# A second chunk of gate and up by seven block products, at 1.25 half-steps a turn, in a four-layer trunk on one core

## The chip, the core and the metric

The program runs on one core of a Trainium2 chip. The metric is the device time of one execution in microseconds. Engines: PE (TensorE, matmuls) with PEld (its weight loads), DVE (VectorE), ACT (ScalarE), POOL (GpSimd) and SP (SyncE, which issues most DMAs). Each engine works through its own instructions in program order and waits on semaphores for the others.

## The reference

A trunk of 4 layers on x of shape (1, 256, 1024) in float32. Each layer is a feed-forward block, a mixer, and a second feed-forward block:

```python
x = x + 0.5 * swiglu(rms_norm(x, g0), w_gate, w_up, w_down)   # 1024 -> 2816 -> 1024
x = x + mixer(rms_norm(x, g1))        # conv, attention (MLA), spatial gating, conv
x = x + 0.5 * swiglu(rms_norm(x, g2), w_gate, w_up, w_down)
# swiglu(x) = (silu(x @ w_gate) * (x @ w_up)) @ w_down
```

The attention mixer is causal softmax attention with 16 heads over low-rank queries and keys (w_uq, w_ukv) and an output matrix w_o. All weights are float32 and every matrix is read once.

## The kernel before, in words

**Precision.** Every float32 product is made of three matmuls. A weight tile is split into a high part (`whi`, a copy on ScalarE, L112) and a low part (`wlo`, a subtraction on VectorE, L123); activations likewise (L291, L292). `products` (L333, L334, L336) then adds high x high, high x low and low x high in PSUM.

**Rows and streams.** The 256 rows are two tiles t = 0 and t = 1 of 128 rows. `stream(t)` is a Python generator that goes through all twelve blocks. `advance(t)` takes one step of it; here one such call is named a turn. The loop at the end (L1281 to L1288) lets t = 0 go `LAG` = 4 turns ahead and then takes t = 1 and t = 0 alternately. The order of instructions on every engine is the order of these calls; nothing is reordered later. `later(n, f)` runs f after n more turns.

**Weight units.** `unit` asks `Weights.get` for a piece of 1024 columns in all (two rows of tiles by 512 columns). Both tiles use one unit; it is made when t = 0 asks for the unit `AHEAD` = 4 places before it (3 while activations are on their way, `CHAIN_AHEAD`). `make` issues the copy on ScalarE in that turn, `complete` the subtraction on VectorE at the start of the next turn, and then SP may load a further raw tile (`N_RAW` = 6 buffers). A plain turn of the feed-forward block is one unit: six matmuls of 512 columns.

**Feed-forward block** (`ffn`, L503). Columns of gate and up come in chunks 0 to 4 of 512 and chunk 5 of 256. For a plain chunk, each tile takes 4 turns of gate and 4 of up (chunk 0 and the gate of chunk 1 go together, in 12 turns: first half of the contraction, then the second). When up is done, `up_done` (L525) multiplies (L532), transposes 32 by 32 (L534) on VectorE, and after every second chunk sends the result through DRAM (`Turned`), from where `read` (H_READ = 7 turns before its use) and `take` (H_TAKE = 2 turns before) bring it back as the left operand of down. The products with down follow in `rows_into_x`; the chunk done by seven products comes last there.

**Seven products.** Except in the very first block, chunk 4 of both tiles is computed as a 2 x 2 block product (rows: the two tiles; contraction: two halves of 512; columns: two halves of 256) with seven block products in place of eight. This is the generator `sevens` (L606), called a lane. It needs sums of activation blocks (`form`, L621), sums of weight blocks (`sum_of`, L650), high and low parts of them (`high` L626, `low` L631), and 12 matmuls of 256 columns per product (L764). One matrix (gate or up) of a chunk is called a unit of the lane here and has steps q = 0 to 6. A product takes two half-steps. The first (up to the `yield` at L752) issues for VectorE the subtraction for the next product, the sum for the one after it, and small additions (L686) that join results; the second issues the 12 matmuls and ScalarE's copy for the product after the next. Five half-steps stand ahead of the first product. Banks y, z, x of PSUM are reused: at q = 6 VectorE reads z (L751, through L686) before the seventh product adds to it.

**Pace of the lane.** The lane is opened when t = 1 enters the block, and starts once all activations are taken. In each turn `beside` (L1271) adds `RATE` = 0.6 to a credit and takes one half-step if the credit has reached 1. `follow` (L580) brings t = 1 up to one turn behind t = 0 at turn 10 of t = 0 (t = 0 stands still for three rounds), and back to four when the lane ends. `load_first` loads the first four weight blocks during the mixer or the block before; further blocks are loaded at q = 4 and q = 5 of the unit before into a pool of four buffers.

**Activations between blocks.** `prepare_x` (L432) sends half of x through DRAM (write, four reads) and takes it `X_TAKE` = 12 turns later on ScalarE (L443, L291) and VectorE (L292).

**Attention.** `mla` (L1051): `keys`, then four `queries`, each with a unit of w_uq (asking four ahead, so units of w_o are made there too), then scores with Exp (L1187), values and the output product.

**Start.** `start` issues 4 warm-up matmuls and, three turns later, `WARM[1]` = 6 more.

## Time and profile before

| | us |
|---|---|
| three runs, median (lowest to highest) | 1853.66 (1853.48 to 1860.08) |
| the profiled execution, its time | 1853.95 |
| its span, first to last instruction | 1852.2 |

The time of an execution is some 1.75 us over its span. In a row of a timeline the first number is the start in us from the span's start, the second the duration; then engine, line, operation, tile written and tiles read, and how many in a row (x4). What stands in brackets is the idle time of the engine just before, and what ended it. Matmuls are pipelined: the spacing of their starts tells their cost, not the duration shown.

### The profile page before, as it was taken

Reading aid. Unit: us, or ns where it says so; the run is one execution under the profiler, and the core shown is the slowest. Engines: PE = TensorE matmul, PEld = TensorE weight load, DVE = VectorE, ACT = ScalarE, POOL = GpSimd, SP = SyncE. Lnnn points to the kernel's source line nnn. Section 1 sums busy time; section 2 is a strip of 40 time slices with the busy share of each in tenths; the row PEclk is TensorE's granted clock in tenths of the full one; section 3 lists DMA queues with packets and bytes.
Section 4 is the critical chain, followed back from the end, with each engine's and each line's share of the span. In section 5 each row is a group of like instructions: output and inputs, shape, how many; then the busy total and the mean of one; then the engine's idle time right before and its main releaser. Section 6 shows DMA issues by size and latency. Waiting matters only on the chain.

```text
span 1852.2 us, 24827 instructions
## 1 busy us (share of the span) xinstructions
PE 1826.1 (99%) x9022; PEld 1521.3 (82%) x9022; DVE 1286.6 (69%) x1574; ACT 988.7 (53%) x1421; POOL 144.7 (8%) x279
## 2 busy tenths in 40 slices
PE   9999999999999989999999999999999999999999
PEld 7888887888888868888878888888888888878887
DVE  5555677776687666686668665778667775777773
ACT  5344545554655486554565456565456554546452
POOL 2000101000530151100010001100000000000000
PEclk9999999999999998999999999999999999999999
DMA  7678666669766841676976786656786777766674
GB/s 265 218 237 238 215 222 199 215 190 293 230 208 204 250 151 58 195 226 192 272 237 220 216 261 204 225 177 225 236 265 202 227 233 230 236 205 188 218 232 132
DMA packets 251612, 400.36 MB, mean 216 GB/s; under 512 B 25415, under 2 KB 116449, under 8 KB 251489
## 3 DMA queue, kind: packets, MB, share of 16 engines
q1 hardware_dynamic: 250480, 397.09, 68.0%
q8 instruction: 70, 1.15, 0.3%
q0 software_dynamic: 608, 1.11, 0.2%
q10 hardware_dynamic: 400, 0.57, 0.1%
q14 instruction: 54, 0.43, 0.1%
HBM read 365.67 MB, written 33.03 MB: 215 GB/s over the span
## 4 chain that ended last, share of the span: by engine, by line
PE 90%; DVE 3%; ACT 2%; DMA 2%; issue 2%; SPq 0%; ACTq 0%; DVEq 0%
PE acc L334 27%; PE acc L336 27%; PE acc L333 27%; PE acc L764 7%; PE tr L299 1%; DMA xturn<-s 1%; DVE wlo L123 1%; ACT whi L112 1%; PE acc L1206 1%; PE acc L1179 1%; DMA raw<-in_ffn_gate_dram 1%; DVE wlo L631 0%; ACT whi L626 0%; DVE s L803 0%; SPq L468 0%
## 5 line engine op out<-in xcount | busy, mean ns | idle before, releaser
L333 PE MATMUL acc<-whi,s 128*128 128x512 f32 (+2 forms) x2440 | 937.8, 384 | 2.4 <-ACT s L291 1.7
L334 PE MATMUL acc<-wlo,s 128*128 128x512 f32 (+2 forms) x2440 | 932.8, 382 | 2.7 <-DVE wlo L123 2.7
L336 PE MATMUL acc<-whi,s 128*128 128x512 f32 (+2 forms) x2440 | 896.5, 382 | 0.0
L123 DVE TENSOR_TENSOR wlo<-raw,whi 128x1024 fp32r<-128x1024 f32 (+1 forms) x580 | 685.7, 1208 | 100.9 <-ACT whi L112 98.4
L112 ACT ACTIVATE whi<-raw 128x1024 fp32r<-128x1024 f32 (+1 forms) x580 | 588.1, 1044 | 87.3 <-DMA raw<-in_ffn_down_dram 43.7
L336 PEld LDWEIGHTS acc<-whi,s 128*128 128x128 f32 x2440 | 459.1, 188 | 96.8 <-DVE s L292 1.0
L334 PEld LDWEIGHTS acc<-wlo,s 128*128 128x128 f32 x2440 | 459.4, 188 | 95.7 <-DVE wlo L123 6.9
L333 PEld LDWEIGHTS acc<-whi,s 128*128 128x128 f32 x2440 | 459.2, 188 | 92.8 <-ACT s L291 2.8
L626 ACT ACTIVATE whi<-block 128x1024 fp32r<-128x1024 f32 x98 | 103.4, 1055 | 130.6 <-DVE block L650 130.6
L764 PE MATMUL acc<-whi,s 128*128 128x256 f32 x784 | 155.4, 281 | 7.5 <-DVE s L686 7.5
L764 PEld LDWEIGHTS acc<-whi,s 128*128 128x128 f32 x784 | 127.0, 188 | 14.2 <-DVE s L686 10.5
L631 DVE TENSOR_TENSOR wlo<-block,whi 128x1024 fp32r<-128x1024 f32 x98 | 118.7, 1212 | 1.2 <-ACT whi L626 0.3
L292 DVE TENSOR_TENSOR s<-s,s 128x512 fp32r<-128x512 f32 (+1 forms) x58 | 39.9, 688 | 113.7 <-ACT s L291 112.3
L523 ACT ACTIVATE s<-acc,evened 128x512 f32<-128x512 f32 (+1 forms) x70 | 44.9, 641 | 128.0 <-PE acc L336 125.8
L411 POOL TENSOR_TENSOR total<-ss,ss 128x1 f32<-128x1 f32 x26 | 8.0, 306 | 1308.2 <-ACT s L402 1308.2
L764 PE MATMUL acc<-wlo,s 128*128 128x256 f32 x392 | 110.0, 281 | 0.0
L402 ACT ACTIVATE s<-x 128x512 bf16<-128x512 f32 x48 | 30.3, 630 | 133.3 <-DVE x L426 98.3
L325 DVE TENSOR_TENSOR s<-big,s 128x512 fp32r<-128x512 f32 x68 | 46.2, 680 | 77.6 <-ACT s L324 74.9
L532 DVE SCALAR_TENSOR_TENSOR s<-acc,evened,s 128x512 f32<-128x512 f32 (+1 forms) x70 | 48.5, 693 | 64.3 <-PE acc L336 64.3
L426 DVE SCALAR_TENSOR_TENSOR x<-acc,x 128x512 f32<-128x512 f32 x32 | 22.0, 689 | 79.8 <-PE acc L336 79.7
L764 PEld LDWEIGHTS acc<-wlo,s 128*128 128x128 f32 x392 | 73.7, 188 | 3.7
L650 DVE TENSOR_TENSOR block<-block,block 128x1024 f32<-128x1024 f32 x56 | 68.4, 1221 | 1.0
(151 smaller groups left out, 904.4 us busy)
## 6 DMA issues: line engine op xcount, KB each, us to landing
raw<-in_ffn_down_dram SPq DMA_DIRECT2D x176, 512.0 KB, 5.8
raw<-in_ffn_gate_dram SPq DMA_DIRECT2D x148, 512.0 KB, 4.5
raw<-in_ffn_up_dram SPq DMA_DIRECT2D x148, 512.0 KB, 4.6
raw<-in_conv_w_in_dram SPq DMA_DIRECT2D x48, 512.0 KB, 5.0
turn<-big SPq DMA_DIRECT2D x32, 512.0 KB, 3.1
big<-turn SPq DMA_DIRECT2D x128, 128.0 KB, 5.9
block<-in_ffn_gate_dram SPq DMA_DIRECT2D x28, 512.0 KB, 6.1
block<-in_ffn_up_dram SPq DMA_DIRECT2D x28, 512.0 KB, 6.7
```

Of the source, the lines that this page charges most:

```text
L112: self.nc.scalar.activation(hi[:, part], self.loaded[u][:, part], AF.Copy)
L123: self.nc.vector.tensor_tensor(out=lo[:, part], in0=src[:, part], in1=hi[:, part].bitcast(F32), op=ALU.subtract)
L325: nc.vector.tensor_tensor(out=lo.rearrange("p k (i b) -> p k i b", b=32), in0=src, in1=hi.bitcast(F32).rearrange("p k (i b) -> p k i b", b ...
L333: nc.tensor.matmul(ps, lhsT=ah[:, k, :], rhs=wh[:, wk, c], start=first, stop=False)
L334: nc.tensor.matmul(ps, lhsT=ah[:, k, :], rhs=wl[:, wk, c], start=False, stop=False)
L336: nc.tensor.matmul(ps, lhsT=al[:, k, :], rhs=wh[:, wk, c], start=False, stop=last)
L523: nc.scalar.activation(sg[n], ps[:, :w], AF.Silu, scale=r)
L532: nc.vector.scalar_tensor_tensor(out=h, in0=ps[:, :w], scalar=r, in1=sg[n], op0=ALU.mult, op1=ALU.mult)
L626: nc.scalar.activation(hi, src, AF.Copy)
L631: nc.vector.tensor_tensor(out=lo, in0=src, in1=hi.bitcast(F32), op=ALU.subtract)
L650: nc.vector.tensor_tensor(out=to, in0=to, in1=raws[u][added[q]], op=ALU.add)
L764: nc.tensor.matmul(ps[:, :256], lhsT=f[:, k, :], rhs=w[:, k, :], start=q in (0, 1, 3) and k + n == 0, stop=k == 3 and n == 2, skip_group_c ...
```

## The change

Chunk 3 joins chunk 4 in the lane (four units in place of two), and the lane takes 1.25 half-steps a turn, so in every fourth turn two. The four raw blocks get a buffer each, by a table that turns with every unit, so that each block of the next unit goes into the buffer that is freed first: block 11 is loaded at q = 3, 12 and 22 at q = 4, 21 at q = 5. Chunks of the lane are read 4 turns before use. Plain chunk 2 is now paired with chunk 5 on its way through DRAM, where one buffer is added. In attention, t = 0 calls Exp once on a scrap element after its normalization; the queries ask for fewer units ahead (4, 3, 2, 1), and units of w_o are made between the scores of t = 0. The second warm-up has 3 matmuls in place of 6.

```diff
-N_SEVENS_RAW = 4
-N_DRAM = 4
+N_DRAM = 5
-H_READ, H_TAKE = 7, 2
-SEVENS, RATE = (4,), 0.6
+H_READ, H_TAKE, SEVENS_READ = 7, 2, 4
+SEVENS, RATE = (3, 4), 1.25
-WARM = (4, 6)
+WARM = (4, 3)
-    sevens_pool = ctx.enter_context(tc.tile_pool(name="sevens", bufs=N_SEVENS_RAW))
+    sevens_pool = ctx.enter_context(tc.tile_pool(name="sevens", bufs=1))
-    def unit(t, m, k, n, c0, width):
+    def unit(t, m, k, n, c0, width, ahead=AHEAD):
...
-        return W.get((m, k, n, c0, width, copy), AHEAD if not any(in_chain) else CHAIN_AHEAD)
+        return W.get((m, k, n, c0, width, copy), min(ahead, AHEAD if not any(in_chain) else CHAIN_AHEAD))
...
-            events.setdefault(at - H_READ, []).append(lambda n=n: read(n))
+            events.setdefault(at - (SEVENS_READ if n in seven else H_READ), []).append(lambda n=n: read(n))
...
+    buffers = {"21": 0, "11": 1, "12": 2, "22": 3}
+    def next_buffers():
+        buffers.update({"11": buffers["21"], "12": buffers["11"], "22": buffers["12"], "21": buffers["22"]})
...
-        raw = sevens_pool.tile([P, 4, 256], F32, tag="block", name=name("block"))
+        raw = sevens_pool.tile([P, 4, 256], F32, tag=f"block{buffers[name_]}", name=name("block"))
...
-        for n, block in enumerate(("11", "12", "22", "21")):
+        for n, block in enumerate(("21", "11", "12", "22")):
...
+            if q == 3:
+                next_buffers()
+                load(u + 1, "11")
             if q == 4:
-                load(u + 1, "11", "12")
+                load(u + 1, "12", "22")
             if q == 5:
-                load(u + 1, "22", "21")
+                load(u + 1, "21")
...
     def mla(t, i, ib, shared, then):
         a, r = yield from normed(t, IDLE_MLA)
+        if t == 0:
+            nc.scalar.activation(tiny(1, "scrap", 1), half, AF.Exp)
...
-            queries(b, unit(t, ("w_uq", ib), 0, 2, 384 * b, 384))
+            queries(b, unit(t, ("w_uq", ib), 0, 2, 384 * b, 384, 4 - b))
...
             later(S_TURN[t], lambda h0=h0, p=p: values(h0, p))
+            if t == 0 and h0 >= 4:
+                W.make()
...
         credit[0] += RATE
-        if credit[0] >= 1:
+        while lanes and credit[0] >= 1:
             credit[0] -= 1
```

## Rows read from the trace of the kernel before

**Rows 1.** The page, part 1: busy time of each engine.

```profile
PE 1826.1 (99%) x9022; PEld 1521.3 (82%) x9022; DVE 1286.6 (69%) x1574; ACT 988.7 (53%) x1421; POOL 144.7 (8%) x279
```

**Rows 2.** The page, part 4: the chain that ended last, by engine.

```profile
PE 90%; DVE 3%; ACT 2%; DMA 2%; issue 2%; SPq 0%; ACTq 0%; DVEq 0%
```

**Rows 3.** Busy time by stretch; columns: us, PE, PEld, DVE, ACT, POOL, PEclk, DMA share, GB/s.

```profile
1410.00:1445.00 35.00, 35.00 (x177) 29.51 (x176) 34.44 (x39) 20.96 (x27) 0.00 (x0) 1.00 0.64 201
```

**Rows 4.** Timeline of TensorE: a product's first matmul, then plain ones.

```profile
1419.63 0.28 PE L764 MATMUL acc<-whi,s 128*128 128x256 f32 x1
...
1421.06 0.39 PE L333 MATMUL acc<-whi,s 128*128 128x512 f32 x1
...
1423.84 0.39 PE L333 MATMUL acc<-whi,s 128*128 128x512 f32 x1
```

**Rows 5.** Timeline of VectorE in the same lane.

```profile
1416.62 0.69 DVE L621 TENSOR_TENSOR s<-s,s 128x512 f32<-128x512 f32 x1
1417.22 1.22 DVE L631 TENSOR_TENSOR wlo<-block,whi 128x1024 fp32r<-128x1024 f32 x1
...
1434.14 1.22 DVE L123 TENSOR_TENSOR wlo<-raw,whi 128x1024 fp32r<-128x1024 f32 x1
1435.28 0.74 DVE L532 SCALAR_TENSOR_TENSOR s<-acc,evened,s 128x512 f32<-128x512 f32 x1
1436.05 0.71 DVE L534 STREAM_TRANSPOSE big<-s 128x512 f32<-128x512 f32 x1
1436.69 1.18 DVE L123 TENSOR_TENSOR wlo<-raw,whi 128x1024 fp32r<-128x1024 f32 x1
```

**Rows 6.** Turn 0 in timelines and chain: sixth lane; then the first lane.

```profile
1404.70 0.69 ACT L523 ACTIVATE s<-acc,evened 128x512 f32<-128x512 f32 x1 [1.83 <-PE acc L336]
1409.42 0.69 DVE L292 TENSOR_TENSOR s<-s,s 128x512 fp32r<-128x512 f32 x1 [5.67 <-ACT s L291]
1419.80 1.42 PE acc L764 x12
...
311.43 0.69 DVE L292 TENSOR_TENSOR s<-s,s 128x512 fp32r<-128x512 f32 x1 [6.65 <-ACT s L291]
324.11 1.42 PE acc L764 x12
```

**Rows 7.** Waits of TensorE (total us, times, longest), then timelines at a seventh product.

```profile
PE acc L764 <- DVE s L686: 7.5, 7, 1.1
...
1456.74 0.41 DVE L686 TENSOR_TENSOR s<-acc,s 128x256 f32<-128x256 f32 x1
1457.21 0.38 PE L764 MATMUL acc<-whi,s 128*128 128x256 f32 x1 [1.04 <-DVE s L686]
```

**Rows 8.** Loads of the lane's weight blocks, 512 KB each.

```profile
DMA to landing us min/median/max: 4.8/6.5/9.0
```

**Rows 9.** Attention: timelines of ScalarE and TensorE, then stretches as in rows 3.

```profile
683.19 1.04 ACT L112 ACTIVATE whi<-raw 128x1024 fp32r<-128x1024 f32 x1
704.18 1.28 ACT L1187 ACT_TABLE_LOAD   x1 [0.76 <-DVE nb L1184]
694.38 1.06 PE L299 MATMUL tr<-ident,s 128*96 128x128 f32 x4 [2.19 <-DVE s L1049]
694.00:696.00 2.00, 1.62 (x7) 1.60 (x8) 1.97 (x5) 1.97 (x5) 1.11 (x2) 0.61 0.03 10
696.00:698.00 2.00, 2.00 (x10) 1.81 (x9) 1.90 (x8) 1.12 (x2) 0.50 (x2) 0.54 0.60 134
```

**Rows 10.** Timeline of the start: second warm-up, then a weight's low part.

```profile
6.09 2.67 PE L266 MATMUL acc<-ident_r 128*128 128x512 f32 x6
7.62 1.28 DVE L123 TENSOR_TENSOR wlo<-raw,whi 128x512 fp32r<-128x512 f32 x2
```

**Rows 11.** DMA issues: kind, count, size each, median us from issue to landing.

```profile
turn<-big SPq DMA_DIRECT2D x32, 512.0 KB, 3.1
...
s<-turn SPq DMA_DIRECT2D x56, 64.0 KB, 4.4
```

## The prediction

> **What bounds the kernel now.** I read the engines' busy time first: TensorE is busy 99% of the span, VectorE 69%, ScalarE 53% [rows 1]. The chain of waits agrees: nine tenths of it is TensorE [rows 2]. So the kernel is a queue of matmuls, and leaving matmuls out is worth their spacing, as long as nothing else ends last. Whether that holds must be read from the stage in which the change puts work, the first part of a feed-forward block, where one chunk runs by seven products beside the plain chunks. There, over 35 us in a row, VectorE is busy 34.4 us [rows 3]. The average of 69% hides a stage in which VectorE is full and TensorE is kept fed only because every product is asked for late.
>
> A turn is one call of `advance`; I number turns from turn 0, in which the last half of the activations is taken and the generator `sevens` (the lane) may begin.
>
> **Matmuls: less.** Twelve plain matmuls of 512 columns start over 2.78 us, 0.232 us each; the twelve of a product, 256 columns, take 1.43 us to the next start [rows 4]. A chunk of gate and up costs 96 x 0.232 = 22.2 us plain and 14 x 1.43 = 20.0 us by products. It saves 2.2 us in each of the seven blocks that have a lane: **15.5 us**. The Trainium skill (TensorE: Matmul & The Clock Gate, "Back-to-back issue gap") speaks against this: sustained streams are given as 131 ns at 512 columns and 81 ns at 128; an estimate on the line between, 98 ns at 256, makes it 14 x 12 x 98 ns = 16.5 us against 12.6 us, a loss of 27 us over seven blocks. The trace shows both shapes, and in it the small one takes half the time of the large one; the measurement decides, and I give that case no chance.
>
> **VectorE: more, and sooner.** From start to start, a subtraction or sum of 1024 elements takes 1.14 us, one of 512 elements 0.60 us, an up chunk's product and transpose 0.77 + 0.64 us [rows 5]. A chunk by products needs 14 subtractions and 8 sums of 1024 where a plain one needs 8 subtractions: 14 x 1.14 = 16 us more per block. Spread evenly it fits. At 1.25 half-steps a turn, a turn holds 1.39 + 0.625 x 1.43 = 2.28 us of TensorE; VectorE has half a weight unit's subtraction (0.57), an up chunk's share (0.18) and 0.625 of a product's share (1.14 + 4/7 x 1.14 + about 0.35 for the operations of 256 elements, taken at half the price of 512; 2.14 in all), so 2.09 us, 92%. What decides is the beginning, where it isn't spread evenly.
>
> Start of the lane. TensorE ended turn 0 when ScalarE's wait in the 1404.70 row ended, while VectorE, held in order behind the activations' trip through DRAM, reached turn 0's subtraction at 1409.42 [rows 6]. The first product is the lane's seventh half-step. At 0.6 it falls in turn 11, at 1.25 in turn 5: six turns or 6 x 1.39 = 8.3 us earlier. Over the seven blocks that subtraction starts 10.4 (the worst) to 12.7 us ahead of the first product, 11.9 in the mean (both ends: [rows 6]), so the new first product is asked for about 3.5 us after it. By then VectorE must have done that subtraction, five operations of 512, two weight units' subtractions and the first block's, 0.6 x 5 to 6 + 3 x 1.14 = 6.5 us: a wait of 3.0 us in the mean, 2.3 to 4.6.
>
> It doesn't end there. The seventh product writes a bank that VectorE reads in the half-step before it (L751), and in VectorE's order that read stands behind the next unit's first subtraction and sum. Even now TensorE waits for it once per block, 7 times 1.1 us at most [rows 7]. At the new rate it is asked for at turn 15: 3.5 + 10 x 1.39 + 6 x 1.43 = 26.0 us after the subtraction of turn 0. Up to and with that read VectorE has: 0.61, eight operations on activations (4.9), eight blocks' subtractions (9.1), six sums (6.8), six weight units (6.8: t = 0 stands still three rounds), two up chunks (2.8), two of 256 elements (0.7) = 31.8 us, and one gap of 1.2 us where a sum must pass ScalarE before its subtraction. 33.0 - 26.0 = 7.0 us, in which the 3.0 are contained; 1.0 of it is paid today. So 6.0 us more per block, **+42 us**; without the gap 4.8 (34 us), with a late block load 6.5 (46 us).
>
> Later units. There are three such unit ends per block in place of one. At the second, count from the end of turn 19, the last matmul of t = 0's second up chunk: VectorE has two up chunks, three blocks, two sums and two weight units, 2 x 1.41 + 7 x 1.14 = 10.8 us; then the freed buffer is loaded, 6.5 us [rows 8]; then sum and read, 1.5 us: 18.8. TensorE has seven turns and four products, 15.5. The bounds are 0 (VectorE comes early, having caught up at the wait before) and 3.3 us; I take 2.0, since the wait before lets it catch up in part: **+14 us** over seven blocks. At the third no up chunk stands in that stretch, and I take 0, with up to 1.5 us for the bound.
>
> **The other edits.** In the attention block ScalarE's chain ends last. Three copies of output weights of 1.04 us leave it, and the table load before the first Exp, 1.28 us, goes to an earlier turn where ScalarE idles; but one of TensorE's waits there, 2.19 us, is for VectorE [rows 9]. Bounds: 0 and 3.1 + 1.3 + 1.3 us (a slow stretch of the clock less). I take the load and half of the copies: **-2.9 us**. The copies land among the scores, where ScalarE waits for VectorE anyway. The Trainium skill (ScalarE: Activation LUTs, "What ACT_TABLE_LOAD costs") counts 2.66 us for a switch, with the drain; this trace shows only the load's row, and by the page the sum would be 1.4 us lower. The three warm-up matmuls less save nothing: the first real ones wait for the low part of their weights, ready after 8.2 us [rows 10]. The later reads of turned chunks (4 turns before use, 2 before the take, at 1.39 us and two streams 5.6 us) give a little less than four issues and 4.4 us to landing take [rows 11], so ScalarE may wait half a microsecond; four weight units made ahead cover it. The read that now follows its write by one turn holds SP's queue for about 3.1 us [rows 11]; six raw buffers cover that; without them it costs 3.1 us per tile. The new block order and the fifth DRAM buffer cost nothing by themselves.
>
> **Sum**, against the profiled execution's 1853.95 us, 0.3 above the median: 1853.95 - 15.5 - 2.9 + 42 + 14 = 1891.5 us, so about **1891 us**.
>
> **Rivals.**
> 1. Faster: VectorE's lead holds. Then 1853.95 - 15.5 - 2.9 = 1835.5 us, 1826 to 1844 with the bounds. For it: in the stage now TensorE loses hardly anything though VectorE is full [rows 3], and on average 92% fits. Against: the order count above. It decides if the subtraction of turn 0 starts some 7 us sooner against TensorE, for example because the activations come back from DRAM earlier. Chance 0.22.
> 2. No change: only the first product waits (7 x 3.0 = 21 us), and VectorE catches up before the seventh: 1853.95 - 18.4 + 21 = 1856.5 us. It needs 4 us of slack in VectorE's order that I don't find. Chance 0.10.
> 3. Slower still, by the clock: after a wait of 2.19 us the granted clock fell to 0.61 and 0.54 in the next 2 us stretches, near the lower of its levels, 1.2 GHz [rows 9]. By those two rows a wait of that length costs 2 x 0.39 + 2 x 0.46 = 1.7 us more. Inside the first unit that is hidden, since VectorE ends last there; behind two unit ends per block it isn't: 1891 + 14 x 1.7 = 1915 us. Chance 0.08.
> 4. The lane does not run at that rate, or the second chunk stays plain: impossible to tell from times alone, but the counts would show it. Chance under 0.01.
>
> **Numbers.** The forecast has 0.60, its own range 1866 (42 -> 34, 14 -> 0) to 1912 (42 -> 46, 14 -> 23, and some 8 at the third unit's end). About 0.5%, 9 us, is what a measurement can tell from no change. Faster 0.22, same 0.10, slower 0.68 (cases 3 and forecast). The range 1836 to 1915 takes in half of case 1 and leaves out its lower half and a little above.
>
> **What would show it.** Plain matmuls of 512 columns fall by 224 on each of L333, L334, L336, and the products' matmuls go from 1176 to 2352. TensorE should wait at the first product of every lane 2 to 5 us for VectorE's subtraction (L631), and some 3 us at the seventh for L686; VectorE should be full for some 60 us from each lane's start. In the attention block the table load should stand before the scores. If TensorE's waits on L764 come to less than 15 us in all, my count of VectorE's order is wrong, and the time is near 1836.

## The result, and the profile after

The changed kernel takes 1943.3 us (median of 4 runs, 1939.4 to 1954.1) where the kernel before took 1855.1 us beside it: a ratio of 1.048, with 1.046 to 1.050 as its 95% interval. That is 88 us slower. The forecast was slower by 37 us; the sign was right and the size was not, and the time lies outside the range. The profiled execution has a span of 1942.7 us, 90.5 us more than before. All line numbers below are those of the kernel after unless said otherwise: the products' matmuls are L772 (before L764), the plain ones L332, L333 and L335, VectorE's low form of a weight block L636, its sum L655, its read of a product's bank L691, ScalarE's snapshot of a bank L687, an up chunk's product and transpose L531 and L533.

The page of the kernel after, busy time and chain of waits by engine, against [rows 1] and [rows 2]:

```profile
PE 1845.5 (95%) x9523; PEld 1552.5 (80%) x9523; DVE 1415.5 (73%) x1721; ACT 1040.9 (54%) x1513; POOL 146.4 (8%) x279
...
PE 39%; DVE 11%; DMA 5%; ACT 4%; issue 3%; SPq 1%; POOL 0%; ACTq 0%; DVEq 0%
```

The shares of the kernel after add up to only 63% of the span, where those before add up to all of it: this chain was not followed back to the start. Of the part that was followed, TensorE has about six tenths (39 of 63) where it had nine, and VectorE 17% (11 of 63) where it had 3%. TensorE no longer ends everything. The groups of the page show that the change did what it says (count behind the x, then busy time and mean ns, then idle time before):

```profile
L332 PE MATMUL acc<-whi,s 128*128 128x512 f32 (+3 forms) x2216 | 854.5, 386 | 4.5 <-ACT whi L111 2.7
L772 PE MATMUL acc<-whi,s 128*128 128x256 f32 x1568 | 324.3, 289 | 54.4 <-DVE s L691 41.1
L772 PE MATMUL acc<-wlo,s 128*128 128x256 f32 x784 | 226.0, 288 | 19.1 <-DVE wlo L636 19.1
```

The plain matmuls went from 2440 to 2216 on each line and the products' to 1568 + 784 = 2352, both as forecast. The idle time is at the products. TensorE's waits (total us, times, longest), where before there was the one line of [rows 7]:

```profile
PE acc L772 <- DVE s L691: 41.1, 21, 3.7
PE acc L772 <- DVE wlo L636: 19.1, 9, 3.2
PE acc L772 <- ACT s L687: 13.3, 19, 1.2
```

These three are 73.5 us, against 7.5 us before. Where in a lane they stand is read from the timeline of TensorE, here the first of the seven lanes: first product (two rows), then the seventh, the fourteenth and the twenty-first, each the last of a unit of seven.

```profile
316.56 0.28 PE L772 MATMUL acc<-whi,s 128*128 128x256 f32 x1
318.94 0.39 PE L772 MATMUL acc<-wlo,s 128*128 128x256 f32 x1 [2.10 <-DVE wlo L636]
...
345.06 0.39 PE L772 MATMUL acc<-whi,s 128*128 128x256 f32 x1 [0.46 <-DVE s L691]
...
373.70 0.38 PE L772 MATMUL acc<-whi,s 128*128 128x256 f32 x1 [2.13 <-DVE s L691]
...
402.95 0.39 PE L772 MATMUL acc<-whi,s 128*128 128x256 f32 x1 [3.73 <-DVE s L691]
```

Over the seven lanes the first product waits 2.08 to 3.21 us, the seventh 0.43 to 0.48, the fourteenth 0.93 to 2.21 and the twenty-first 3.68 to 3.73; the twenty-eighth, which ends the lane, doesn't wait. A wait of the trace is a little less than what is lost: in the first two rows the starts are 2.38 us apart where 0.12 us is usual, so 2.26 us are lost for 2.10 shown, 0.16 us more at every wait.

The longest wait takes the clock with it. Two stretches of the kernel after, around the twenty-first product (columns as in [rows 3]; PEclk is the third from the right):

```profile
400.00:405.00 5.00, 2.05 (x13) 2.05 (x14) 4.96 (x6) 2.34 (x3) 0.00 (x0) 0.90 0.82 297
405.00:410.00 5.00, 5.00 (x35) 5.00 (x34) 1.39 (x2) 0.99 (x3) 0.00 (x0) 0.76 0.34 108
```

TensorE stood idle for 3.73 us, VectorE was full, and then the granted clock fell to its lower level: 0.10 x 5 + 0.24 x 5 = 1.7 us of TensorE's time are lost. I call 1 less the granted clock, summed over stretches of 1 us, the lost clock. Within the span it is 32.4 us in the kernel after (mean clock 0.983) and 7.2 us before (0.996); an expectation below counts 18.0 us for a run that has 17.1, because it goes past the last instruction. Of the 32.4, 23.9 lie in the lanes, 14 falls of 1.7 us: 7 behind the twenty-first product, one in every lane; 6 behind the first product, in five lanes; 1 behind a fourteenth. The other 8.5 lie in the attention part.

### The profile page after: what moved, and what is told of

It is laid out like the page before. It is cut to its first block, busy times and chain, and to the rows that moved or that the text cites. A ratio compares the mean times of both kernels' runs of the same rounds, so it can differ in the third digit from the quotient of the medians.

```text
span 1942.7 us, 26046 instructions
## 1 busy us (share of the span) xinstructions
PE 1845.5 (95%) x9523; PEld 1552.5 (80%) x9523; DVE 1415.5 (73%) x1721; ACT 1040.9 (54%) x1513; POOL 146.4 (8%) x279
## 3 DMA queue, kind: packets, MB, share of 16 engines
q8 instruction: 74, 1.21, 0.3%
## 4 chain that ended last, share of the span: by engine, by line
PE 39%; DVE 11%; DMA 5%; ACT 4%; issue 3%; SPq 1%; POOL 0%; ACTq 0%; DVEq 0%
PE acc L335 10%; PE acc L332 10%; PE acc L333 10%; PE acc L772 6%; DVE wlo L636 3%; DVE block L655 2%; DVE wlo L122 2%; DMA block<-in_ffn_gate_dram 1%; DMA block<-in_ffn_up_dram 1%; ACT whi L111 1%; DMA xturn<-s 1%; PE tr L298 1%; DMA raw<-in_ffn_down_dram 1%; DVE s L531 1%; ACT whi L631 1%
## 5 line engine op out<-in xcount | busy, mean ns | idle before, releaser
L332 PE MATMUL acc<-whi,s 128*128 128x512 f32 (+3 forms) x2216 | 854.5, 386 | 4.5 <-ACT whi L111 2.7
L333 PE MATMUL acc<-wlo,s 128*128 128x512 f32 (+3 forms) x2216 | 847.9, 383 | 2.7 <-DVE wlo L122 2.7
L335 PE MATMUL acc<-whi,s 128*128 128x512 f32 (+3 forms) x2216 | 811.8, 382 | 0.0
L122 DVE TENSOR_TENSOR wlo<-raw,whi 128x1024 fp32r<-128x1024 f32 (+2 forms) x524 | 620.7, 1208 | 63.5 <-ACT whi L111 63.4
L111 ACT ACTIVATE whi<-raw 128x1024 fp32r<-128x1024 f32 (+2 forms) x524 | 530.6, 1042 | 76.7 <-DMA raw<-in_ffn_down_dram 49.2
L335 PEld LDWEIGHTS acc<-whi,s 128*128 128x128 f32 x2216 | 420.4, 190 | 89.2 <-DVE s L324 2.3
L332 PEld LDWEIGHTS acc<-whi,s 128*128 128x128 f32 x2216 | 422.0, 190 | 84.6 <-ACT whi L111 4.5
L333 PEld LDWEIGHTS acc<-wlo,s 128*128 128x128 f32 x2216 | 421.3, 190 | 81.5 <-DVE wlo L122 5.5
L772 PE MATMUL acc<-whi,s 128*128 128x256 f32 x1568 | 324.3, 289 | 54.4 <-DVE s L691 41.1
L631 ACT ACTIVATE whi<-block 128x1024 fp32r<-128x1024 f32 x196 | 207.0, 1056 | 286.1 <-DVE block L655 279.7
L772 PEld LDWEIGHTS acc<-whi,s 128*128 128x128 f32 x1568 | 261.6, 194 | 76.8 <-DVE s L691 48.6
L636 DVE TENSOR_TENSOR wlo<-block,whi 128x1024 fp32r<-128x1024 f32 x196 | 237.2, 1210 | 46.9 <-ACT whi L631 46.2
L772 PE MATMUL acc<-wlo,s 128*128 128x256 f32 x784 | 226.0, 288 | 19.1 <-DVE wlo L636 19.1
L772 PEld LDWEIGHTS acc<-wlo,s 128*128 128x128 f32 x784 | 152.1, 194 | 26.9 <-DVE wlo L636 21.8
L655 DVE TENSOR_TENSOR block<-block,block 128x1024 f32<-128x1024 f32 x112 | 136.7, 1221 | 10.4 <-DMA block<-in_ffn_gate_dram 8.7
L323 ACT ACTIVATE s<-s 128x512 fp32r<-128x512 f32 x28 | 17.6, 630 | 86.0 <-DMA s<-turn 86.0
```

What stands on the lines that cost most here:

```text
L111: self.nc.scalar.activation(hi[:, part], self.loaded[u][:, part], AF.Copy)
L122: self.nc.vector.tensor_tensor(out=lo[:, part], in0=src[:, part], in1=hi[:, part].bitcast(F32), op=ALU.subtract)
L332: nc.tensor.matmul(ps, lhsT=ah[:, k, :], rhs=wh[:, wk, c], start=first, stop=False)
L333: nc.tensor.matmul(ps, lhsT=ah[:, k, :], rhs=wl[:, wk, c], start=False, stop=False)
L335: nc.tensor.matmul(ps, lhsT=al[:, k, :], rhs=wh[:, wk, c], start=False, stop=last)
L631: nc.scalar.activation(hi, src, AF.Copy)
```

## The experiments

Three theories stood at the start. **Order**: the loss is a read that frees a bank, standing behind other work in VectorE's order. **Total**: VectorE simply has too much to do in the lane, in whatever order. **Other edits**: part of the loss has nothing to do with the second chunk.

### The other edits alone

```
-SEVENS, RATE = (3, 4), 1.25
+SEVENS, RATE = (4,), 0.6
```

> The changed kernel with one chunk in the lane at 0.6 half-steps a turn again; block order, early Exp, output units, warm-up and DRAM buffer stay changed. Theory (the other edits are worth only the attention block's 2.8 us): 1851 us, within 4. Rival (one of them, such as the block loads or the later output units, carries part of the loss): 1862 or more.

Measured: 1870.5 us, ratio 1.009 (1.006 to 1.012). The rival was right: about 15 us come from the other edits. The lanes are as before, one wait of 1.06 us each. What is new are waits of plain matmuls, in TensorE's view of waits:

```profile
PE acc L332 <- ACT s L323: 6.8, 4, 3.8
```

and behind them, in ScalarE's view of the same run, a wait for a DMA (before, its waits for that read came to 15.4 us in 10):

```profile
ACT s L323 <- DMA s<-turn: 60.6, 14, 8.6
```

This is the turned chunk being read 4 turns ahead of its use in place of 7. Undoing that edit on top of the first run:

```
-H_READ, H_TAKE, SEVENS_READ = 7, 2, 4
+H_READ, H_TAKE, SEVENS_READ = 7, 2, 7
```

> One chunk by seven products at 0.6 half-steps a turn with all other edits, as in the run of the other edits alone (1870.5 us), but the turned tiles of the product chunk are read again 7 turns ahead of their use, as before the change, in place of 4. Theory: the 15 us that the other edits cost are mostly this read: ScalarE waits for its DMA (60.6 us in 14 waits there, longest 8.6), the split that a plain matmul needs comes late (6.8 us in 4 waits of the matmuls at L332), and the granted clock falls after the longest of them (3.4 us lost at 454 to 462). With 7 turns the four waits go and that fall with them: 1860 us (1857 to 1864). Rival: the order of the weight units in the attention layer and the order of the block loads carry the loss, and the read is hidden: 1868 to 1872, with the waits at L332 below 3 us all the same.

Measured: 1857.6 us (10 runs), ratio 1.001 (1.000 to 1.002). As the theory said: the waits for L323 are gone from TensorE's list, ScalarE's waits for the read are 14.9 us, and the time is that of the kernel before. This run still has the edits of the attention part, so with one chunk all edits but the later read come to between 0 and 4.5 us together; what each gives or costs is not told apart. By the two medians the later read costs 13 us with one chunk; the four times of the first run spread over 12 us (1867.8 to 1879.5).

### The rate without the second chunk

```
-SEVENS, RATE = (3, 4), 1.25
+SEVENS, RATE = (4,), 1.25
```

> One chunk in the lane, at 1.25 half-steps a turn. Theory (VectorE's order at the start of the lane decides, whatever the number of chunks): TensorE waits some 2.6 us at each lane's first product, 1 to 2 us in the rest of the first unit, the clock falls in about half of the lanes: 1880 us, 1870 to 1888. Rival (the second chunk's 16 us of VectorE work per block makes the waits): 1851 us, within 4.

Measured: 1901.7 us, ratio 1.024 (1.023 to 1.026), 31 us above the run of the other edits at 0.6 and 46 us above the kernel before; the theory's range ended at 1888. The 31 us are likely too little for the rate, since the later read no longer shows: TensorE has no wait for L323 here, as it has none in the kernel after. From turn 0's subtraction to the seventh product it takes 32.9 us in the mean of the lanes, as in the kernel after (32.8). The waits stand where they stand in the kernel after, and none of them is at a twenty-first product, since there is none:

```profile
PE acc L772 <- DVE wlo L636: 18.2, 8, 3.2
PE acc L772 <- ACT s L687: 13.1, 21, 1.2
PE acc L772 <- DVE s L691: 4.1, 7, 1.3
```

### The read that frees the bank, issued first

```
+            if q == 6:
+                add(vs[1][:, 256:], z, v3, ALU.subtract)
             if s + 1 <= last:
                 low(s + 1)
             sum_of(s + 2)
...
-            elif q == 6:
-                add(vs[1][:, 256:], z, v3, ALU.subtract)
```

> The changed kernel with the read of bank z at q = 6 issued ahead of the next unit's subtraction and sum in place of behind them. Theory (the seventh product waits because of what stands ahead of that read, 2.3 us): the waits of 0.5, 1.7 and 3.7 us at the three unit ends fall to 0, 0 and 1.4 us, and the clock no longer falls at the third: 1900 us, 1890 to 1910. Rival (VectorE is simply full, the wait moves to the next product's low part): 1932 us or more.

Measured: 1889.7 us, ratio 1.018 (1.017 to 1.020), just under the theory's range of 1890 to 1910: 54 us come back for moving one instruction of 0.4 us per unit. The waits for it fell from 41.1 us in 21 to:

```profile
PE acc L772 <- DVE s L691: 9.6, 7, 1.7
```

They are all at the twenty-first product; those at the seventh and fourteenth are gone, and so are the falls of the clock behind the third unit (lost clock 17.1 us). Visible waits give 31.5 us, the lost clock 15 us, the unseen 0.16 us at 14 waits 2 us: 49 of the 54.

The same move in the **kernel before**, where it is the only wait of the products (its `if q == 6` goes ahead of `low(s + 1)` in the same way):

```
+            if q == 6:
+                add(vs[1][:, 256:], z, v3, ALU.subtract)
             if s + 1 <= last:
                 low(s + 1)
```

> The kernel before, with one thing moved: at each unit's last product the VectorE instruction that reads the z accumulator (the add that frees it) is issued ahead of the next low form and the next block sum, not behind them. Theory: the only wait of the products in the kernel before (7.5 us in 7, 1.06 each at the seventh product of a lane's first unit) is the read standing behind other work in VectorE's order, so it goes: 1855.5 - 7.5 = 1848 us (1846 to 1850). Rival: VectorE's work before the next product is the same, and the low form that the next product needs comes late in place of the read: 1855 (1853 to 1857), with a wait of about 1 us moved to the product after it.

Measured: 1846.9 us, ratio 0.9952 (0.9939 to 0.9964): 9 us faster than the kernel before. No wait of a product is left in any of the seven lanes; the low form behind the read had room. Seven waits of 1.06 + 0.16 us are 8.5 us. This version beats both kernels.

### Faster still, and later

```
-SEVENS, RATE = (3, 4), 1.25
+SEVENS, RATE = (3, 4), 1.5
```

> The changed kernel at 1.5 half-steps a turn. Theory (order and pace): the first product is asked one turn earlier, 1.4 us more per lane, and a unit gives VectorE 23 us in place of 25.6: 1955 to 2000 us. Rival (only VectorE's total work counts, and it is the same): 1943 us, within 6.

Measured: 1941.1 us, ratio 1.046 (1.043 to 1.048). The time fits the rival, that VectorE's total counts, and my theory of 1955 us and more fails. At the higher rate waits grow at the second product (up to 1.8 us) and at the seventh (1.8 to 2.7 us) and nearly go at the twenty-first (at most 1.3 us). All waits at the products come to 62 us in place of 73.5, and those of plain matmuls for the two splits (L122, L323) to 12.5 us in place of 2.7, so the sum stays near 75 us.

```
+            credit[0] = -5.0
...
-SEVENS, RATE = (3, 4), 1.25
+SEVENS, RATE = (3, 4), 1.5
```

with the read issued first as well:

> Two chunks by products as in the kernel after, at 1.5 half-steps a turn, each lane beginning 5 half-steps of credit (some four turns) later than its blocks are there, and the read of z issued ahead of the low form at each unit's last product. Theory: what is left in the run with the read first (1889.7 us) is set by order, not by VectorE's total: the first product's 18 us are the first forms made in the same turn as the product that needs them. With the start late nothing changes in that, as forms and first product still come in one turn: first-product waits stay near 2 to 3 us, and the higher rate puts waits of 1 to 1.8 us on the second and third products: 1895 to 1915 us. Rival: the delay lets VectorE drain its queue before the first product, its wait goes below 0.7 us a lane, and with the clock falls behind it gone the time is 1865 to 1885.

Measured: 1945.2 us, ratio 1.048 (1.045 to 1.051); neither case gave the time. The first product waits as expected (1.8 to 3.2 us), but 42.4 us in 31 waits for L636 stand at products throughout the lane. The likely reason, not tested: a lane that begins later and goes faster only packs VectorE's work more densely.

Then the lane with its forms made at the same time as in the read-first run and only its products later:

```
+        for _ in range(2):
+            yield
         pending = []
```

> Two chunks at 1.25 with the read first (1889.7 us), and two empty half-steps between a lane's first forms and its first product: the forms are made when they are made now, the product comes 1.6 turns, some 2.2 us, later. Theory: the first product's wait (18.3 us in 8, 2.1 to 3.2 each) is VectorE's work since turn 0 against the time at which the product is asked for, as in the prediction's count, so 2.2 us of each go, and with them the falls of the clock behind the longer ones (some 8 of the 18.0 us lost there): 1889.7 - 15 - 8 = 1867 us (1860 to 1873). Rival: VectorE's order has no slack behind it, so the wait moves to the later products: 1880 to 1892, with the waits of L772 for VectorE still 20 us or more.

Measured: 1883.6 us, ratio 1.015 (1.013 to 1.017): 6 us back, not 22. The rival held. The first product's wait is gone (0 to 0.6 us), and the second now waits 2.6 to 3.1 us in every lane for its own low form:

```profile
PE acc L774 <- DVE wlo L636: 21.7, 13, 3.1
```

So behind the first product's subtraction there is no slack in VectorE's order: the start of the lane is limited by how much VectorE has to do there, not by one late instruction. That is the opposite of the read of the bank, where moving one instruction was enough.

The same with the early reads:

```
-H_READ, H_TAKE, SEVENS_READ = 7, 2, 4
+H_READ, H_TAKE, SEVENS_READ = 7, 2, 7
```

> As the run with two empty half-steps, with the turned tiles of the product chunks read 7 turns ahead, not 4. With one chunk at 0.6 this gave back 13 us (1870.5 to 1857.6). Theory: with two chunks no wait of a plain matmul for ScalarE's take shows among TensorE's waits, since the turns are longer there and the take has more time, so it gives nothing: within 3 us of the run without it. Rival: the reads' waits of ScalarE (86.6 us in 24) cost there too, through the split of weights behind them: 8 to 13 us faster than the run without it.

Measured: 1877.7 us, ratio 1.012 (1.010 to 1.014), 6 us below the run without it, between the two expectations; the intervals of the two ratios still touch. The 2.8 us of plain matmuls' waits for L323 went, and the lost clock fell from 19.2 to 13.9 us. By the medians the later read costs this version less than half of what it costs with one chunk.

### Is the fall of the clock a cost of its own?

Three runs put spare matmuls ahead of a product that waits.

```
+            if s == last:
+                for n in range(24):
+                    nc.tensor.matmul(ps[:, 256:], lhsT=ident_r, ...)
```

> The kernel after, with 24 more matmuls of 256 columns ahead of each lane's last product, into the half of the accumulator bank that nothing uses: about 24 x 0.12 = 2.9 us of TensorE work that lies in the 3.7 us in which the last product waits for VectorE's read, at 7 lanes. They compute nothing that is used. Theory: the granted clock falls by half for some 3.4 us behind each of these 7 waits because TensorE stood idle, and this costs about 1.7 us a lane on top of the wait; with the wait filled the wait left is about 0.8 us, the clock doesn't fall there and 7 x 1.7 = 12 us come back: 1943.3 - 12 = 1931 us (1928 to 1935). Rival: at the low clock other engines set the time, since TensorE waits for them anyway, and the fall is hidden: 1943 (1940 to 1946), with the waits elsewhere longer. Second rival: the added matmuls run longer than the wait or delay others: above 1946.

Measured: 1970.5 us, ratio 1.062 (1.061 to 1.064). The run does not answer the question: I had put the matmuls ahead of the lane's last product, the twenty-eighth, and the 3.7 us are at the twenty-first. 24 matmuls of 2.9 us in seven lanes are 20 us of plain extra work, and the waits are nearly as they were.

```
-            if s == last:
+            if s == 20:
```

> The 24 spare matmuls of the filled-end run (24 x 0.12 = 2.9 us) put where the 3.7 us wait is: ahead of the 21st of a lane's 28 products, the end of its third unit, not ahead of the 28th. They write the half of the bank that nothing reads. Theory: the granted clock falls behind these 7 waits because TensorE stood idle, and that costs 1.7 us a lane beside the wait; filled, the wait left is some 0.8 us, the clock stays up there, and 7 x 1.7 = 12 us come back: 1943.3 - 12 = 1931 us (1928 to 1935). Rival: at the low clock TensorE only runs into VectorE's next wait later, so the fall is hidden: 1943 (1940 to 1947), with the falls gone all the same.

Measured: 1967.3 us, ratio 1.060 (1.058 to 1.062). This is far above both expectations, and the timeline of TensorE in the first lane says why:

```profile
404.48 4.44 PE L772 MATMUL acc<-ident_r 128*128 128x256 f32 x24 [3.73 <-DVE s L691]
408.72 0.41 PE L776 MATMUL acc<-whi,s 128*128 128x256 f32 x1
```

The spare matmuls waited 3.73 us for the same read, though they write the other half of the bank. They ran behind the wait, at the low clock: 4.24 us from start to start where the run before had 2.86 us for the same 24. So the fall does stretch what comes next; whether that reaches the end was still open.

```
-                    nc.tensor.matmul(ps[:, 256:], lhsT=ident_r, ...)
+                    nc.tensor.matmul(x[:, 256:], lhsT=ident_r, ...)
```

> The 24 spare matmuls ahead of the 21st product once more, now into the unused half of the bank of x, which VectorE has read two half-steps earlier, so that they needn't wait for the read of z (in the run before they stood behind that wait: 3.73 us, then 4.24 us of spare matmuls at the low clock). Theory: TensorE runs through, 2.9 of the 3.7 us are filled, the granted clock stays up behind the 7 third unit ends, and 7 x 1.7 = 12 us come back: 1943.3 - 12 = 1931 us (1927 to 1935). Rival: the 12 us are hidden behind VectorE's next waits: 1941 to 1946, with the falls gone all the same.

Measured: 1937.1 us, ratio 1.045 (1.043 to 1.046). In the first lane, spare matmuls and twenty-first product in the timeline:

```profile
398.81 3.03 PE L772 MATMUL acc<-ident_r 128*128 128x256 f32 x24
402.70 0.39 PE L776 MATMUL acc<-whi,s 128*128 128x256 f32 x1 [0.87 <-DVE s L691]
```

and the stretch around them, columns as in [rows 3]:

```profile
398.00:410.00 12.00, 11.13 (x95) 10.93 (x94) 9.38 (x11) 4.18 (x6) 0.00 (x0) 1.00 0.65 227
```

Now it is filled: VectorE's read comes when it came, the wait left is 0.87 us, and the clock stays at 1.00. All seven falls there are gone, and TensorE takes 25.4 to 25.6 us from the twenty-first to the twenty-eighth product where it took 27.0 to 27.1: 1.6 us back in every lane, 11 us in all, on the spot. Some other falls came: behind fourteenth products (three in place of one) and in the attention part (10.2 us lost against 8.5). Net, the lost clock fell by 6.4 us, from 32.4 to 26.0, and the profiled span by 5.9 us, from 1942.7 to 1936.8, with useless work in the same place. The time lies between the two expectations; the 12 us of the theory were not reached, as the falls moved. The intervals of the two ratios touch (1.046 to 1.050 against 1.043 to 1.046), so I take this as support, not proof.

Each execution has its mean granted clock, and these say that a lost microsecond doesn't always reach the end. The mean clock of four executions rose from 0.983 in the kernel after to 0.990 here, some 14 us of lost clock less, for 6 us of median time. In the run with the read first the four executions have clocks of 0.991, 0.994, 0.992 and 0.997, 17 to 6 us lost, and their times lie within 3.0 us (1887.6 to 1890.6).

### Work taken from VectorE

```
-                nc.vector.tensor_tensor(out=to, in0=to, in1=raws[u][added[q]], op=ALU.add)
+                nc.gpsimd.tensor_tensor(out=to, in0=to, in1=raws[u][added[q]], op=ALU.add)
```

> Two chunks at 1.25 with the read first (1889.7 us), and the sums of weight blocks, 16 in a lane, on GpSimd in place of VectorE. Theory: VectorE's work in its order is what ends last, so 16 x 1.14 = 18 us a lane leave it; the first product's wait stays (2.1 to 3.2 us; no sum stands ahead of its subtraction), the waits at the 21st product (9.6 us in 7) go: 1889.7 - 9.6 = 1880 us (1874 to 1884). Rival: GpSimd's sum of 1024 elements takes well over the 1.14 us of VectorE (its rows here show no wide one), ScalarE's high form waits for it, and the subtraction behind that comes later than now: above 1892, with TensorE's waits for VectorE at L772 longer than 28 us.

Measured: 2022.7 us, ratio 1.090 (1.088 to 1.093): the rival. In the other run the four combinations of activations (L626) went to GpSimd in the same way:

```
-            nc.vector.tensor_tensor(out=f, in0=x, in1=y, op=op)
+            nc.gpsimd.tensor_tensor(out=f, in0=x, in1=y, op=op)
```

> As the run with the read first (1889.7 us), with the four combinations of activations that begin a lane (512 elements each, three of them ahead of the first product's subtraction) on GpSimd. Theory: the first product waits for VectorE's work since turn 0, so 3 x 0.6 = 1.8 us of each of the 7 waits go, and the falls of the clock behind them (8.5 us lost): 1889.7 - 12.6 - 8.5 = 1869 us (1865 to 1876). Rival, as in the run with two empty half-steps: the second product then waits for its own subtraction, since VectorE has no slack behind the first: 1878 to 1890. Second rival: GpSimd is slower at it by more than the 1.8 us, and ScalarE and the first product wait for it: above 1891.

Measured: 1904.5 us, ratio 1.026 (1.025 to 1.028): the second rival, 15 us slower than the read first alone; the seven first products wait 31.7 us, 4.5 each. Both operations are far slower on GpSimd. Groups by line of the first run, then of the second:

```profile
L655 POOL TENSOR_TENSOR block<-block,block 128x1024 f32<-128x1024 f32 x112 | 304.5, 2729 | 557.2 <-DVE wlo L636 193.6 <-issue 128.6 <-DMA block<-in_ffn_up_dram 119.8
```

```profile
L626 POOL TENSOR_TENSOR s<-s,s 128x512 f32<-128x512 f32 x28 | 47.7, 1724 | 77.7 <-ACT s L442 77.1
```

A sum takes 2.73 us where VectorE takes 1.22, a combination 1.72 us where VectorE takes 0.69. So these two runs could not take work off VectorE without adding a longer one, and the theory of VectorE's total was not tested by them in the direction in which I meant it.

### The attention part alone

The kernel before with the read first and the three edits of the attention part (table load early, query weights asked for later, output weights made among the scores):

```
+        if t == 0:
+            nc.scalar.activation(tiny(1, "scrap", 1), half, AF.Exp)
...
+            queries(b, unit(t, ("w_uq", ib), 0, 2, 384 * b, 384, 4 - b))
...
+            if t == 0 and h0 >= 4:
+                W.make()
```

> The kernel before with the read of z issued first at a unit's end (1846.9 us), and with the change's three edits of the attention part alone: the early table load, the query weights asked for 4 to 1 units ahead, the output weights made among the scores. Theory: these edits are what the prediction took them for, 2.9 us, measured in the kernel after as 2.7 us from the first row of the attention part to the next lane: 1844 us (1842.5 to 1845.5). Rival: as a lane at 0.6 follows and the weights made among the scores meet it, they give nothing or cost: 1846.5 to 1850.

Measured: 1845.5 us, ratio 0.9944 (0.9932 to 0.9956), not told apart from the 1846.9 us without these edits. The stretch itself is clearer: from the first copy of the attention part (L1055 before, L1065 after) to the subtraction in turn 0 of the next lane, in the kernel before, the kernel after and this run, one row from each:

```profile
664.90:783.63 118.73, 110.38 (x628) 94.98 (x627) 78.36 (x165) 79.36 (x179) 34.18 (x52) 0.94 0.42 137
```

```profile
690.00:814.30 124.30, 112.99 (x628) 96.85 (x627) 78.62 (x165) 77.94 (x177) 32.45 (x52) 0.93 0.40 131
```

```profile
664.90:781.36 116.46, 106.60 (x628) 90.72 (x627) 78.23 (x165) 77.77 (x178) 32.45 (x52) 0.99 0.43 139
```

The same 628 matmuls take 118.7 us before, 116.5 us with the edits, and 124.3 us in the kernel after, which has the same edits. With the one-chunk kernel read at 7 turns it is 116.4 us. So the stretch is 2.2 us shorter with the edits, but the clock differs too: the lost clock of the stretch is 6.8 us before, 1.7 us in this run and 8.5 us in the kernel after. How much of the 2.2 us is the edits' own is therefore not told apart, and the lost clock by itself doesn't explain the kernel after, which takes 5.6 us more than the kernel before with 1.7 us more of it. The 2.7 us that the expectation takes from the kernel after were misread: they run to the lane's first product, which comes six turns earlier there. What sets off the falls there no run shows. Nor is the clock the same in all executions of one kernel: the five of this run have a mean of 0.999 four times and 0.995 once, and the slowest time (1850.1 us) is the one at 0.995.

## Why the prediction was right in sign and wrong in size

**The account.** From turn 0's subtraction in one lane to that in the next, the six sections and the two ends add 90.5 us in the two profiled executions. 5.6 us of these lie in the attention part; the other 84.9 are 12.1 us a block. The prediction's terms against what was found, over the seven blocks:

| term | forecast | found |
|---|---|---|
| matmuls | -15.5 | about -17 (counts as forecast, a product 1.42 us) |
| lane start to the first unit's end | +42 | about +38 |
| second unit's end | +14 | about +21 |
| third unit's end | 0 | about +39 |
| attention part | -2.9 | +5.6 |
| the rest | 0 | about +4 |

**What bounds the kernel, and the saving.** Right. VectorE full beside a busy TensorE [rows 3] was the thing to see, and the product's matmuls kept their spacing: twelve take 1.42 us when nothing is waited for.

**Lane start.** The mechanism was right, and each size close. From the timeline of VectorE in the first lane: turn 0's subtraction, the first block's subtraction, the read at the seventh product.

```profile
312.38 0.69 DVE L291 TENSOR_TENSOR s<-s,s 128x512 fp32r<-128x512 f32 x1 [6.65 <-ACT s L290]
...
317.67 1.22 DVE L636 TENSOR_TENSOR wlo<-block,whi 128x1024 fp32r<-128x1024 f32 x1
...
344.59 0.41 DVE L691 TENSOR_TENSOR s<-acc,s 128x256 f32<-128x256 f32 x1
```

The block's subtraction ends 6.5 us after the first row's start (forecast 6.5), in all lanes but one, which has 6.7. The first product is asked for 3.0 to 4.2 us after it, 3.7 in the mean (3.5), and waits 2.6 us in the mean (3.0). The read ends 32.6 us after it (33.0). The seventh product starts at 32.8 in the mean; without waits it would start at 3.7 + 10 x 1.39 + 6 x 1.43 = 26.2, so 6.6 us are lost (7.0), less some 1.2 us of today: 5.4 a block, 38 us. Two things inside it were not as told. VectorE is busy 51.8 of the 60 us from 312 to 372 us, not full for all of them. And only 0.46 us stand at the seventh product, not 3, because ScalarE's snapshots (8.3 us in 12 waits of the first unit, of which the prediction says nothing) and the fall of the clock behind the first product take the time earlier. VectorE ends last either way, so they don't add to it, as the third rival had said of the first unit.

**Second unit's end.** The mechanism was right, the size a little low. The sum ahead of the read waits for the load of its block in every lane, 0.6 to 1.9 us; in the first:

```profile
372.09 1.23 DVE L655 TENSOR_TENSOR block<-block,block 128x1024 f32<-128x1024 f32 x1 [1.78 <-DMA block<-in_ffn_gate_dram]
```

The loss is 1.7 us in the mean at the fourteenth product, 0.7 us for a snapshot at the thirteenth, 0.3 us unseen, and one fall of the clock: 3.0 a block against 2.0, inside the bounds of 0 to 3.3.

**Third unit's end: the step that failed.** The prediction put it so: "At the third no up chunk stands in that stretch, and I take 0, with up to 1.5 us for the bound." VectorE's timeline ahead of the read shows both up chunks in that very stretch:

```profile
395.05 0.75 DVE L531 SCALAR_TENSOR_TENSOR s<-acc,evened,s 128x512 f32<-128x512 f32 x1 [1.40 <-PE acc L335]
395.84 0.71 DVE L533 STREAM_TRANSPOSE big<-s 128x512 f32<-128x512 f32 x1
396.48 1.18 DVE L636 TENSOR_TENSOR wlo<-block,whi 128x1024 fp32r<-128x1024 f32 x1
397.58 1.22 DVE L122 TENSOR_TENSOR wlo<-raw,whi 128x1024 fp32r<-128x1024 f32 x1
398.71 0.74 DVE L531 SCALAR_TENSOR_TENSOR s<-acc,evened,s 128x512 f32<-128x512 f32 x1
399.49 0.71 DVE L533 STREAM_TRANSPOSE big<-s 128x512 f32<-128x512 f32 x1
400.12 1.18 DVE L636 TENSOR_TENSOR wlo<-block,whi 128x1024 fp32r<-128x1024 f32 x1
401.34 1.22 DVE L655 TENSOR_TENSOR block<-block,block 128x1024 f32<-128x1024 f32 x1
402.48 0.42 DVE L691 TENSOR_TENSOR s<-acc,s 128x256 f32<-128x256 f32 x1
```

The first L531 cannot begin before TensorE has finished the up chunk's matmuls (1.40 us of waiting), and from there on the order is fixed: two chunks with their transposes, two block subtractions, one of weights, one sum, and only then the 0.42 us that TensorE waits for. The twenty-first product is asked for 3.7 us before that. I had not placed the next up chunk in turns, though the prediction's own numbers do: t = 0's second up chunk ends with turn 19, the next one sixteen turns later (four of gate and four of up, the two tiles in turn), with turn 35, and at 1.25 the twenty-first product falls in turn 37. From there the count that I had made for the second end gives 2 x 1.41 + 4 x 1.14 + 0.4 = 7.8 us of VectorE against two turns and one product, 4.2 us, of TensorE: 3.6 us, where 3.7 were measured. The wait is 3.7 us, its unseen part 0.16 and the fall of the clock behind it 1.7: 5.6 us a block, 39 us. The run with the read first shows that it was this order: the up chunks stay ahead, only the read goes ahead of the subtraction and the sum, and the wait falls to 1.2 to 1.7 us and the fall behind it goes.

**Clock.** The third rival's price of 1.7 us per fall is what the trace shows, and its place was half right: it had two unit ends per block, and it was one end per block, in every lane, and a fall behind a fourteenth product once. Its term belonged into the forecast with the wait that it follows, not into a rival of 8%; how much of it reaches the end is shown in part only, by the filled wait above.

**The other edits.** The attention part was to give 2.9 us. With its edits alone the stretch is 2.2 us shorter, not told apart from its clock, and in the kernel after it is 5.6 us longer, for which no step of mine held a reason. The later reads were costed at nothing: "ScalarE may wait half a microsecond; four weight units made ahead cover it". In the run of the other edits ScalarE waits 60.6 us for them, up to 8.6 us at a time, and the cover is too small by 3.8 us at the worst place: 13 us with one chunk at 0.6. In the kernel after ScalarE waits 86.0 us for them in 24 waits, but no wait of TensorE for L323 is left, so there the cover held. For the remaining edits see the run that reads at 7 turns: 0 to 4.5 us with the attention edits in it.

**Rivals and range.** The faster case is refuted by the waits above, 73.5 us at the products. The range ended at 1915 because it took the third unit's end as 0 to 1.5 us a block where 5.6 were found, and the attention part as a gain of 0 to 5.7 us where 5.6 were lost. The lower end of the forecast's own range has a slip: 42 -> 34 and 14 -> 0 take 1891.5 to 1869.5, not 1866.

Of the three theories at the start, **order** holds for the unit ends, where one moved read gave 54 us back. **Total** holds for the lane's start, where the wait only went over to the second product when the first was put off. Of **other edits**, the 13 us found with one chunk do not show in the kernel after.

What stays open: why the attention part holds its clock in some executions and not in others, why it takes longer in the kernel after, and whether VectorE's work at a lane's start could be thinned enough for a second chunk to pay. In the best version with two chunks here, read first, pause and early reads, it did not: 1877.7 us, against 1845.5 us for the best with one.

## What to carry to other kernels

When one engine is full in a stretch, its average share says nothing; write its order out up to every instruction that frees a buffer for the bound engine, once for each place where that happens, and don't carry the count of one place over to the next. An instruction that frees a buffer belongs first in its step: moving one of 0.4 us gave 54 us in the slower kernel and 9 us in the tuned one. And a wait of the bound engine is priced with the clock that it loses behind it, here up to 1.7 us on top of 3.7.

## What the runs showed of the hardware

The sums on GpSimd did more than take 2.73 us each: they held VectorE up. In the run with the sums, two sums in a row on GpSimd, then VectorE beside them:

```profile
325.18 6.08 POOL L655 TENSOR_TENSOR block<-block,block 128x1024 f32<-128x1024 f32 x2 [2.43 <-DVE wlo L636]
...
325.01 1.22 DVE L122 TENSOR_TENSOR wlo<-raw,whi 128x1024 fp32r<-128x1024 f32 x1
326.15 2.89 DVE L636 TENSOR_TENSOR s<-s,s 128x512 fp32r<-128x512 f32 x1
```

A subtraction of 512 elements took 2.89 us; all 28 of that kind have a mean of 1.78 us there and 0.69 us in the run with the read first, and the subtractions of 1024 (L636) went from 1.21 to 1.42 us. The Trainium skill (SBUF — State Buffer, "SBUF: two separate sides") says that a VectorE operation with two SBUF inputs and a GpSimd operation that reads SBUF take a shared pair of ports in turn, each for its whole instruction, while the other waits. The trace agrees: the instruction that was already under way (1.22 us) kept its length, the next one took four times its usual 0.69 us. So moving an operation to an idle GpSimd doesn't free VectorE for its duration when VectorE's next operations have two inputs.
